# Hybrid decoder block, state-space stage: a second place for the input tile of the group products, and its load as a step of its own

## The chip, the cores and the metric

The kernel runs on one core of one Trainium2 chip. The metric is device time in microseconds (us) of one execution of the program; several executions are compared by their median.

## What is computed

One decoder block on x of shape 1 x 1024 x 1024 (float32) with a memory of 256 tokens. Two branches read one normalised input: a diagonal state-space recurrence in 32 groups of 16 channels, and an attention with forgetting. Sigmoid gates merge them. A projection, a cross-attention into the memory, a feed-forward layer and a last norm follow. Cut to what matters here:

```python
u = rms_norm(h, norm_mix[l])
proj = u @ w_in[l]
u_ssm, q, k, v, f_logit, gate_logits = jnp.split(proj, [...], axis=-1)
y_ssm = jax.nn.gelu(s5_ssm(u_ssm, lam_re[l], lam_im[l], log_dt[l], b_re[l], b_im[l],
                           c_re[l], c_im[l], d_skip[l]))
...
gate_a, gate_b = jnp.split(jax.nn.sigmoid(gate_logits), 2, axis=-1)
...
# s5_ssm: bu = b_bar * u per group, states by a linear recurrence over the sequence,
# y = Re(c * states) + d_skip * u
```

## The kernel before

Every large product is made of three TensorE products of a high and a low part of each factor (lines 168, 169 and 170), so that a product of two 1024-long factors for 128 output rows and 512 columns is 24 instructions. Weights come by a DMA from HBM into a tile `raw` and are split by ScalarE (`whi`, line 178) and VectorE or GpSimd (`wlo`, line 179).

The stage before this one (`stage_in`) makes the normalised input and the state-space input, and writes the latter to a DRAM tensor `u_d`, one piece for each quarter q of the 32 groups, out of SBUF tiles called `us` (line 435).

`stage_ssm` weaves two things. The main row is 32 gate products (`gate(j, h)`, 24 TensorE instructions each): their sums are passed through a sigmoid into one of two tiles `gs`, and stored to `gate_d` by a DMA that ScalarE issues (line 472). Their weights, a pair of `raw` tiles for every four gate products, are loaded by SP's DMA queue (line 153). Into this row the table `todo` puts the steps of the state-space part, four quarters q = 0 to 3, seven gate products apart:

- ahead of gate product 4 + 7q, `turn_weights(q)`: transposes of the weights `fre` and `fim` (line 1330) which ScalarE copies into `F` (line 1331), 8 small products (line 1336), and a tile `Ts` that is filled by three DMAs in a chain (line 1343).
- ahead of 5 + 7q, `states(q, u_d)`: it takes the one place of the tile `xg` (128 x 1024 float32, 512 KB), loads it from `u_d[q]` on SP's queue (line 1354) and multiplies it at once with `F` in 16 TensorE instructions (line 1361, two for each of eight groups). VectorE and GpSimd turn the result through a rotation, a scan and a rotation back into the states `St` (lines 1369 to 1390). GpSimd clears `St`'s first column (line 1384).
- in the same place `weights(q + 1)` prepares the next quarter's tables, most of it on GpSimd, the last doublings of `EC` and `ES` on VectorE (lines 1279 to 1320).
- ahead of 9 + 7q, `out(q)`: 32 instructions of `xg` with `Tt` (line 1404) and `St` with `Gm` (line 1405), GELU and a split, and `store(q)`: two DMAs to `y_d` (line 1413).

The tile `xg` is read twice, by `states(q)` and by `out(q)`; with one place, the next quarter's load can't start before `out(q)` has read it. The order in which each engine takes its instructions is fixed when the program is built. DMAs of one queue are issued by SP one after the other: an issue that waits for a semaphore holds up those behind it. The tiles of this stage lie in a pool `qp`, in memory that the tiles of `stage_in` (`xt`, `us` and others) held before: the first use of a tile waits for the last reader of what lay there.

Of the kernel before, what the change touches and what calls it, by code (L numbers as in the profile page):

```python
# [451 lines left out]
def stage_ssm(B, s5, qp, uT, w_in, gate_d, u_d, y_d):  # L452

    A, S = B.A, B.S
    s5.qp = qp
    w = {}

    def gate_weights(p):

        w[p] = [B.wblock(w_in, 4 * n, 4, C_G + 256 * p, 256) for n in range(2)]  # L460

    def gate(j, h):
        if h == 0 and j % 2 == 0 and j < 14:
            gate_weights(j // 2 + 1)
        ps = B.bank()
        o = j % 2 * P
        for k in range(8):
            wh, wl = [t_[:, k % 4, o:o + P] for t_ in w[j // 2][k // 4]]
            B.mm3(ps, wh, wl, *uT.rhs(k, h), k == 0, k == 7)
        gs = qp.tile([P, 512], F32, tag="gs", bufs=2, name="gs")  # L470
        mark.append(A.activation(gs, ps, AF.Sigmoid))
        A.dma_start(gate_d[j * P:(j + 1) * P, 512 * h:512 * h + 512], gs)

    def toeplitz():
        with B.tc.issue_after(mark[-1].ins):
            s5.toeplitz()

    def weights(q):
        with B.tc.issue_after(s5.doubled.ins):
            s5.weights(q)  # L480

    mark = []
    gates = [lambda j=j, h=h: gate(j, h) for j in range(16) for h in range(2)]
    gate_weights(0)
    s5.weights(0)
    todo = {}
    for q in range(4):
        todo[4 + 7 * q] = [lambda q=q: s5.turn_weights(q)]
        todo[5 + 7 * q] = [lambda q=q: s5.states(q, u_d)] + ([lambda q=q: weights(q + 1)] if q < 3 else [])
        todo[8 + 7 * q] = [toeplitz]  # L490
        todo[9 + 7 * q] = [lambda q=q: s5.out(q), lambda q=q: s5.store(q, y_d)]
    for i, f in enumerate(gates):
        for g in todo.get(i, []):
            g()
        f()
# [615 lines left out]
class S5:  # L1111
# [5 lines left out]
    def __init__(self, B, sp, lam_re, lam_im, log_dt, b_re, b_im, c_re, c_im, d_skip):  # L1117
        self.B, self.sp = B, sp
        self.raw = (lam_re, lam_im, log_dt, b_re, b_im, c_re, c_im, d_skip)

    def load(self, part):

# [132 lines left out]
    def t2(self, name, bufs=1):  # L1255
        return self.qp.tile([P, 512], F32, tag=f"q_{name}", bufs=bufs, name=name)
# [4 lines left out]
    def weights(self, q):  # L1261

        B, t2 = self.B, self.t2
        V, A, G = B.V, B.A, B.G
        j4 = slice(4 * q, 4 * q + 4)

        def bpow(tab, n):
            return tab[:, :n, j4].rearrange("p k j -> p j k").unsqueeze(3).to_broadcast([P, 4, n, 16])

        def bvec(v, n):  # L1270
            return v[:, j4, :].unsqueeze(2).to_broadcast([P, 4, n, 16])


        self.fb = [t2("fre"), t2("fim")]
        fv = [t_.rearrange("p (j t n) -> p j t n", j=4, t=8) for t_ in self.fb]
        w1, w2 = t2("w1"), t2("w2")
        w1v, w2v = [w[:, :448].rearrange("p (j t n) -> p j t n", j=4, t=7) for w in (w1, w2)]
        for o, (bx, by), op in ((0, (0, 1), ALU.subtract), (1, (1, 0), ALU.add)):
            G.tensor_tensor(out=w1v, in0=bpow(self.ld[0], 7), in1=bvec(self.bb[bx], 7), op=ALU.mult)
            G.tensor_tensor(out=w2v, in0=bpow(self.ld[1], 7), in1=bvec(self.bb[by], 7), op=ALU.mult)  # L1280
            G.tensor_tensor(out=fv[o][:, :, 0:7, :], in0=w1v, in1=w2v, op=op)
            G.tensor_copy(fv[o][:, :, 7, :], self.bb[o][:, j4, :])


        Gm = self.slot("Gm", 2)
        self.Gm = Gm.rearrange("p (g t m) -> p g t m", g=8, t=8)
        Gp = Gm.rearrange("p (j two t m) -> p j two t m", two=2, t=8, m=16)
        gv = [w.rearrange("p (j t m) -> p j t m", j=4, t=8) for w in (w1, w2)]
        for o in range(2):
            G.tensor_tensor(out=gv[0], in0=bpow(self.la[0], 8), in1=bvec(self.cT[o], 8), op=ALU.mult)  # L1290
            G.tensor_tensor(out=gv[1], in0=bpow(self.la[1], 8), in1=bvec(self.cT[1 - o], 8), op=ALU.mult)
            for two in range(2):
                h = slice(64 * two, 64 * two + 64)
                dst = Gp[64 * o:64 * o + 64, :, two]
                if o == 0:
                    V.tensor_sub(dst, gv[0][h], gv[1][h])
                else:
                    V.scalar_tensor_tensor(out=dst, in0=gv[0][h], scalar=-1.0, in1=gv[1][h],
                                           op0=ALU.mult, op1=ALU.subtract)


        EC, ES = [t2(n).rearrange("p (j c) -> p j c", j=4) for n in ("EC", "ES")]
        G.memset(EC[:, :, 0:1], 1.0)
        G.memset(ES[:, :, 0:1], 0.0)
        for k in range(7):
            n = 1 << k
            E = V if k > 4 else G
            bc = lambda tab: tab[:, 7 + k, j4].unsqueeze(2).to_broadcast([P, 4, n])
            for dst, (x1, x2), op in ((EC, (EC, ES), ALU.subtract), (ES, (ES, EC), ALU.add)):
                a1, a2 = [t2(s).rearrange("p (j c) -> p j c", j=4)[:, :, :n] for s in ("d1", "d2")]  # L1310
                E.tensor_tensor(out=a1, in0=x1[:, :, :n], in1=bc(self.cs), op=ALU.mult)
                E.tensor_tensor(out=a2, in0=x2[:, :, :n], in1=bc(self.sn), op=ALU.mult)
                done = E.tensor_tensor(out=dst[:, :, n:2 * n], in0=a1, in1=a2, op=op)
                if E is G:
                    self.doubled = done
        self.EC, self.ES = [e.rearrange("p j c -> p (j c)") for e in (EC, ES)]
        r8 = t2("r8")
        r8v = r8.rearrange("p (j c) -> p j c", j=4)
        A.copy(r8v, self.r8[:, j4].unsqueeze(2).to_broadcast([P, 4, P]))
        G.memset(r8v[:, :, 0:1], 0.0)  # L1320
        self.r8t = r8
# [25 lines left out]
        self.Tt = self.slot("Tt").rearrange("p (g t m) -> p g t m", g=8, t=8)  # L1347
        self.B.ordered = self.B.A.copy(self.Tt.rearrange("p g t m -> p t g m"), self.Ts)

    def states(self, q, u_d):  # L1350
        B, t2 = self.B, self.t2
        V, A, G, T, S = B.V, B.A, B.G, B.T, B.S
        self.xg = self.slot("xg").rearrange("p (g c) -> p g c", g=8)
        S.dma_start(self.xg, u_d[q].rearrange("t (n g) c -> (t n) g c", g=8))

        z = [t2("zre"), t2("zim")]
        zv = [t_.rearrange("p (j c) -> p j c", j=4) for t_ in z]
        for b in range(2):
            ps = B.bank("pv")
            for g in range(4):  # L1360
                T.matmul(ps[:, g * P:(g + 1) * P], self.F[:, 4 * b + g].rearrange("p r s -> p (r s)"),
                         self.xg[:, 4 * b + g, :], start=True, stop=True)
            pr = ps.rearrange("p (j two c) -> p j two c", j=2, two=2)
            for r in range(2):
                for two in range(2):
                    A.copy(zv[r][64 * two:64 * two + 64, 2 * b:2 * b + 2, :], pr[64 * r:64 * r + 64, :, two, :])

        a1, a2, a3, a4 = t2("m1"), t2("m2"), t2("m3"), t2("m4")
        V.tensor_mul(a1, z[0], self.EC)
        G.tensor_mul(a2, z[1], self.ES)  # L1370
        V.tensor_mul(a3, z[1], self.EC)
        V.tensor_mul(a4, z[0], self.ES)
        V.tensor_add(a1, a1, a2)
        V.tensor_sub(a3, a3, a4)
        sr, si = t2("zre"), t2("zim")
        V.tensor_tensor_scan(out=sr, data0=self.r8t, data1=a1, initial=0.0, op0=ALU.mult, op1=ALU.add)
        V.tensor_tensor_scan(out=si, data0=self.r8t, data1=a3, initial=0.0, op0=ALU.mult, op1=ALU.add)
        a1, a2, a3, a4 = t2("m1"), t2("m2"), t2("m3"), t2("m4")
        V.tensor_mul(a1, sr, self.EC)
        G.tensor_mul(a2, si, self.ES)  # L1380
        V.tensor_mul(a3, si, self.EC)
        V.tensor_mul(a4, sr, self.ES)
        self.St = self.slot("St").rearrange("p (g c) -> p g c", g=8)
        G.memset(self.St[:, :, 0:1], 0.0)
        Sv = self.St.rearrange("p (j two) c -> p j two c", two=2)
        for two in range(2):
            h = slice(64 * two, 64 * two + 64)
            v3 = lambda t_: t_[h].rearrange("p (j c) -> p j c", j=4)[:, :, 0:P - 1]
            V.tensor_sub(Sv[0:64, :, two, 1:P], v3(a1), v3(a2))
            V.tensor_add(Sv[64:128, :, two, 1:P], v3(a3), v3(a4))  # L1390
        self.use = (self.xg, self.Gm, self.St)
# [419 lines left out]
```

## Time and profile before

| | |
|---|---|
| three executions | 1586.69, 1590.88, 1595.57 us; median 1590.88 |
| profiled execution | span 1592.0 us from the first to the last instruction; no time of its own beside the span is given |
| TensorE busy | 1538.3 us, 97% of the span |
| VectorE, ScalarE, GpSimd busy | 1023.0, 655.8, 257.4 us |
| granted TensorE clock, mean | 0.984 |
| DMA | 240.86 MB, 151 GB/s over the span |
| state-space stage with the gate products | from about 108 to 328 us |

The profile is one execution, recorded by the hardware. A row of the timeline gives the start, the duration, the engine (PE is TensorE, DVE is VectorE, ACT ScalarE, POOL GpSimd; SPq and ACTq are DMA issues), the line of the kernel and the tiles, written first, then read; in brackets stands the idle time of the engine just before it and what ended it. Where an instruction waits for several semaphores, the one that came last by the profile is named. In rows of stretches, PEclk is the share of full clock that TensorE was granted.

### The profile page before, as it was taken

The numbers are of one execution on the slowest core, as the hardware profiler recorded it, in microseconds if no ns is written. First come the engines' busy times: TensorE is split into PE (matmuls) and PEld (weight loads), VectorE is DVE, ScalarE is ACT, GpSimd is POOL, SyncE is SP. The second block draws the span as 40 slices with busy tenths as digits, with TensorE's granted clock in tenths as the row PEclk, the third lists the DMA queues.
The fourth block names the chain that finished last, engine by engine and source line by source line (L and its number), as shares of the span: only waits on it lengthen the run. The fifth ranks groups of instructions, "written<-read, shape, count | busy, mean of one in ns | idle before, by whom it ended". The sixth has DMA issues, their size and how long they took to land.

```text
span 1592.0 us, 20434 instructions
## 1 busy us (share of the span) xinstructions
PE 1538.3 (97%) x7313; PEld 1265.5 (79%) x7313; DVE 1023.0 (64%) x1822; ACT 655.8 (41%) x1173; POOL 257.4 (16%) x339
## 2 busy tenths in 40 slices
PE   7799989999999899999999989999999999999997
PEld 6688878898777578878888778888888888788885
DVE  6756535444688777776455687777777775565555
ACT  6423334322566553232335564333333333354342
POOL 3037453200121114210001200010000000000001
PEclk8999999999999999999999999999999999999999
DMA  8763556332022746457403176555544443896542
GB/s 293 150 110 96 134 107 125 84 144 29 13 57 46 198 110 200 132 178 257 154 22 98 53 272 237 160 166 167 164 159 158 159 149 129 277 392 223 191 153 106
DMA packets 197941, 240.86 MB, mean 151 GB/s; under 512 B 35448, under 2 KB 126488, under 8 KB 197328
## 3 DMA queue, kind: packets, MB, share of 16 engines
q1 hardware_dynamic: 191216, 223.84, 47.7%
q10 hardware_dynamic: 6624, 15.73, 2.6%
q8 instruction: 57, 0.93, 0.2%
q14 instruction: 44, 0.36, 0.1%
HBM read 165.60 MB, written 75.86 MB: 152 GB/s over the span
## 4 chain that ended last, share of the span: by engine, by line
PE 79%; DVE 7%; DMA 6%; ACT 3%; POOL 2%; issue 2%; SPq 1%; DVEq 0%; POOLq 0%; ACTq 0%
PE mm L868 15%; PE mm L168 8%; PE mm L169 8%; PE mm L170 8%; PE pv L868 7%; PE mm L1005 4%; PE sc L868 4%; PE sc L168 3%; PE sc L170 3%; PE sc L169 3%; PE sc L1005 3%; PE pv L1005 3%; PE misc L1005 1%; DMA raw<-in_w_in_dram 1%; DMA raw<-in_w_mem_kv_dram 1%
## 5 line engine op out<-in xcount | busy, mean ns | idle before, releaser
L178 ACT CAST whi<-raw 128x1024 fp32r<-128x1024 f32 (+2 forms) x124 | 116.0, 941 | 178.0 <-PE mm L868 48.6
L179 DVE TENSOR_TENSOR wlo<-raw,whi 128x1024 fp32r<-128x1024 f32 (+2 forms) x121 | 130.9, 1086 | 75.2 <-ACT whi L178 73.1
L168 PE MATMUL mm<-uh,whi 128*128 128x512 f32 x344 | 138.5, 403 | 2.2 <-ACT whi L178 2.2
L170 PE MATMUL mm<-uh,wlo 128*128 128x512 f32 x344 | 135.9, 396 | 0.5 <-DVE wlo L179 0.5
L169 PE MATMUL mm<-ul,whi 128*128 128x512 f32 x344 | 136.4, 397 | 0.0
L179 DVE TENSOR_TENSOR ol<-or,oh 128x1024 fp32r<-128x1024 f32 x73 | 89.3, 1224 | 70.8 <-ACT oh L178 69.6
L178 ACT CAST oh<-or 128x1024 fp32r<-128x1024 f32 x73 | 76.8, 1053 | 103.3 <-PE mm L1005 35.2
L900 POOL TENSOR_TENSOR g<-a,c 128x512 f32<-128x512 f32 x22 | 35.3, 1603 | 392.8 <-ACT a L899 392.8
L197 POOL TENSOR_TENSOR r<-ms,mhalf 128x1 f32<-128x1 f32 (+1 forms) x30 | 17.9, 597 | 373.0 <-DVE ms L193 345.6
L168 PEld LDWEIGHTS mm<-uh,whi 128*128 128x128 f32 x344 | 66.0, 192 | 14.9 <-ACT whi L178 2.7
L170 PEld LDWEIGHTS mm<-uh,wlo 128*128 128x128 f32 x344 | 65.5, 190 | 14.9 <-DVE wlo L179 1.5
L1630 POOL TENSOR_TENSOR pl<-pf,ph 128x512 fp32r<-128x512 f32 (+1 forms) x32 | 37.8, 1181 | 244.5 <-DVE ph L1629 174.6
L169 PEld LDWEIGHTS mm<-ul,whi 128*128 128x128 f32 x344 | 65.8, 191 | 11.1
L1627 ACT ACTIVATE pf<-sc 128x512 f32<-128x512 f32 (+1 forms) x96 | 46.3, 489 | 44.9 <-DVE sc L1623 29.2
L868 PE MATMUL pv<-S3h,we 128*128 128x512 f32 x176 | 58.1, 389 | 0.0
L1633 DVE TENSOR_TENSOR pl<-pf,ph 128x512 fp32r<-128x512 f32 (+2 forms) x64 | 36.2, 567 | 10.1 <-ACT ph L1632 9.3
L1100 POOL TENSOR_TENSOR sg<-sg,ga 128x512 f32<-128x512 f32 x16 | 29.9, 1890 | 73.3 <-DVE sg L1093 73.0
L1005 PE MATMUL mm<-oh 128*128 128x512 f32 x106 | 41.2, 389 | 0.0
L1005 PE MATMUL mm<-ol,oh 128*128 128x512 f32 x106 | 41.2, 389 | 0.0
L1005 PE MATMUL mm<-oh,ol 128*128 128x512 f32 x106 | 41.2, 389 | 0.0
L168 PE MATMUL sc<-uh,whi 128*128 128x512 f32 x104 | 40.9, 393 | 0.0
L168 PE MATMUL mm<-yh,whi 128*128 128x512 f32 x104 | 40.7, 392 | 0.0
(579 smaller groups left out, 4558.3 us busy)
## 6 DMA issues: line engine op xcount, KB each, us to landing
or<-c_d SPq DMA_DIRECT2D x77, 256.0 KB
raw<-in_w_in_dram SPq DMA_DIRECT2D x22, 512.0 KB
wo<-in_w_ffn_out_dram SPq DMA_DIRECT2D x22, 512.0 KB
c_d<-g SPq DMA_DIRECT2D x44, 256.0 KB
t_d<-wo SPq DMA_DIRECT2D x44, 256.0 KB
or<-t_d SPq DMA_DIRECT2D x44, 256.0 KB
raw<-in_w_ffn_in_dram SPq DMA_DIRECT2D x20, 512.0 KB
rawb<-in_w_ffn_in_dram SPq DMA_DIRECT2D x20, 512.0 KB
```

Of the source, the lines that this page charges most:

```text
L168: T.matmul(ps, lh, rh, start=first, stop=False)
L169: T.matmul(ps, lh, rl, start=False, stop=False)
L170: T.matmul(ps, ll, rh, start=False, stop=last)
L178: self.A.copy(hi, src)
L179: (self.G if pool_lo else self.V).tensor_sub(lo, src, f32(hi))
L868: T.matmul(ps, l_[:, k, :], r_, start=first and k == 0 and i == 0, stop=k == 3 and i == 2, skip_group_check=True)
L900: G.tensor_mul(g[:, 512:], a1, c1)
L1005: T.matmul(ps, l_[:, gi], r_[:, 512:], start=n < 3 and p == 0 and k == 0 or n == 7 and p == 0 and k == 0, stop=p == NP - 1 and k == 2, ski ...
L1100: self.B.G.tensor_mul(self.out[j][:, cs], self.out[j][:, cs], ga)
L1627: self.exp = A.activation(pf[:, off:], ps[:, off:], AF.Exp)
L1630: G.tensor_sub(pl[:, off:], pf[:, off:], f32(ph[:, off:]))
L1633: V.tensor_sub(pl[:, off:], pf[:, off:], f32(ph[:, off:]))
```

## The change

The tile `xg` gets two places. Its load becomes a step `fetch(q)` of its own, which `todo` puts ahead of gate product 1 for q = 0 and ahead of gate product 6 + 7q for quarter q + 1, six gate products before `states(q + 1)`. `states` takes the tile that `fetch` left. No instruction of TensorE, VectorE, ScalarE or GpSimd is added or removed, and as many DMAs are issued as before.

```diff
     gate_weights(0)
     s5.weights(0)
-    todo = {}
+    todo = {1: [lambda: s5.fetch(0, u_d)]}
     for q in range(4):
         todo[4 + 7 * q] = [lambda q=q: s5.turn_weights(q)]
-        todo[5 + 7 * q] = [lambda q=q: s5.states(q, u_d)] + ([lambda q=q: weights(q + 1)] if q < 3 else [])
+        todo[5 + 7 * q] = [lambda q=q: s5.states(q)] + ([lambda q=q: weights(q + 1)] if q < 3 else [])
+        if q < 3:
+            todo[6 + 7 * q] = [lambda q=q: s5.fetch(q + 1, u_d)]
         todo[8 + 7 * q] = [toeplitz]
...
         self.raw = (lam_re, lam_im, log_dt, b_re, b_im, c_re, c_im, d_skip)
+        self.xgs = {}
...
-    def states(self, q, u_d):
+    def fetch(self, q, u_d):
+
+        self.xgs[q] = self.slot("xg", 2).rearrange("p (g c) -> p g c", g=8)
+        self.B.S.dma_start(self.xgs[q], u_d[q].rearrange("t (n g) c -> (t n) g c", g=8))
+
+    def states(self, q):
         B, t2 = self.B, self.t2
         V, A, G, T, S = B.V, B.A, B.G, B.T, B.S
-        self.xg = self.slot("xg").rearrange("p (g c) -> p g c", g=8)
-        S.dma_start(self.xg, u_d[q].rearrange("t (n g) c -> (t n) g c", g=8))
-
+        self.xg = self.xgs.pop(q)
```

Line numbers of the changed kernel are 3 higher from line 1120 on, and 6 higher behind `fetch`.

On SP, at quarters 0 and 1 (`xg_1376` and `xg_1792` are the tiles of q = 0 and q = 1, `raw` are gate weights, `us_648` is the last of the four `us` tiles), the queue stood so before:

```order
L435 DMA u_d_77<-us_648 128x8x128
L153 DMA raw_1616<-in_w_in_dram 128x4x256
L1354 DMA xg_1376<-u_d_77 128x1024
L153 DMA raw_1940<-in_w_in_dram 128x4x256
L153 DMA raw_1946<-in_w_in_dram 128x4x256
L1343 DMA Ts_1330<-Ts_1330 112x128
L1343 DMA Ts_1330<-Ts_1330 96x256
L1343 DMA Ts_1330<-Ts_1330 64x512
L153 DMA raw_2096<-in_w_in_dram 128x4x256
L153 DMA raw_2102<-in_w_in_dram 128x4x256
L1354 DMA xg_1792<-u_d_77 128x1024
L1413 DMA y_d_78<-yh_1650 128x1024
```

and in the changed kernel, where `xg_1224`, `xg_1552` and `xg_1980` are the tiles of q = 0, 1 and 2:

```order
L1356 DMA xg_1224<-u_d_77 128x1024
L1356 DMA xg_1552<-u_d_77 128x1024
L153 DMA raw_1940<-in_w_in_dram 128x4x256
L153 DMA raw_1946<-in_w_in_dram 128x4x256
L1346 DMA Ts_1332<-Ts_1332 112x128
L1346 DMA Ts_1332<-Ts_1332 96x256
L1346 DMA Ts_1332<-Ts_1332 64x512
L153 DMA raw_2098<-in_w_in_dram 128x4x256
L153 DMA raw_2104<-in_w_in_dram 128x4x256
L1356 DMA xg_1980<-u_d_77 128x1024
L1419 DMA y_d_78<-yh_1652 128x1024
```

The load of q = 0 has kept its place. That of q = 1 follows it directly, and where it stood before, behind two pairs of weight loads, that of q = 2 stands now.

On SP one quarter later, before, with `xg_2220` the tile of q = 2:

```order
L153 DMA raw_2396<-in_w_in_dram 128x4x256
L153 DMA raw_2402<-in_w_in_dram 128x4x256
L153 DMA raw_2552<-in_w_in_dram 128x4x256
L153 DMA raw_2558<-in_w_in_dram 128x4x256
L1354 DMA xg_2220<-u_d_77 128x1024
L1413 DMA y_d_78<-yh_2066 128x1024
```

and in the changed kernel, with `xg_2396` the tile of q = 3:

```order
L153 DMA raw_2398<-in_w_in_dram 128x4x256
L153 DMA raw_2404<-in_w_in_dram 128x4x256
L153 DMA raw_2554<-in_w_in_dram 128x4x256
L153 DMA raw_2560<-in_w_in_dram 128x4x256
L1356 DMA xg_2396<-u_d_77 128x1024
L1419 DMA y_d_78<-yh_2068 128x1024
```

The load in this place is now that of the last quarter, and the place where `xg_2648` (q = 3) stood before, a quarter later, is empty.

On GpSimd, in the preparation of quarter 0 (`weights(0)`; what an instruction waits for stands in brackets, Pool_49 is GpSimd's own work), before:

```order
L1311 TENSOR_TENSOR d1_1111<-EC_1107,trg_cs_867 128x4 [waits Pool_49]
L1312 TENSOR_TENSOR d2_1112<-ES_1108,trg_sn_866 128x4 [waits Pool_49]
L1384 MEMSET St_1420 128x8
L1339 MEMSET Ts_1758 128x896
L1281 TENSOR_TENSOR fim_1087<-w1_1088,w2_1089 128x4x112 [waits Pool_49]
L1313 TENSOR_TENSOR EC_1107<-d1_1111,d2_1112 128x4 [waits Pool_49]
```

and in the changed kernel:

```order
L1314 TENSOR_TENSOR d1_1111<-EC_1107,trg_cs_867 128x4 [waits Pool_49]
L1315 TENSOR_TENSOR d2_1112<-ES_1108,trg_sn_866 128x4 [waits Pool_49]
L1390 MEMSET St_1420 128x8 [waits DMAHW4_49]
L1342 MEMSET Ts_1760 128x896
L1284 TENSOR_TENSOR fim_1087<-w1_1088,w2_1089 128x4x112 [waits Pool_49]
L1316 TENSOR_TENSOR EC_1107<-d1_1111,d2_1112 128x4 [waits Pool_49]
```

The order is the same, but the first clearing of `St` has a wait that it had not: the second place of `xg` has moved the tiles behind it in the pool, `St` lies now where `us_648` lay, and DMAHW4_49 tells of the landing of the store of that tile to `u_d`. No other engine's order differs between the two kernels.

## The prediction

> **What bounds the kernel now.** First the page: how busy each engine is, and the chain of waits.
>
> ```profile
> span 1592.0 us, 20434 instructions
> ...
> PE 1538.3 (97%) x7313; PEld 1265.5 (79%) x7313; DVE 1023.0 (64%) x1822; ACT 655.8 (41%) x1173; POOL 257.4 (16%) x339
> ...
> PE 79%; DVE 7%; DMA 6%; ACT 3%; POOL 2%; issue 2%; SPq 1%; DVEq 0%; POOLq 0%; ACTq 0%
> ```
>
> TensorE is the bound, and time is to be had only where it stands still or runs at a reduced clock. So next its waits in the stretch from 100 to 330 us, the stage that the change touches (engine and line, whom it waited for, us in total, times, longest):
>
> ```profile
> PE pv L1361 <- DMA xg<-u_d: 4.9, 1, 4.9
> PE pv L1361 <- ACT whi L178: 0.9, 1, 0.9
> ```
>
> These are all its waits there, and both stand ahead of line 1361, the first products of `xg`. TensorE's timeline around the four quarters' products:
>
> ```profile
> 136.81 1.95 PE L1361 MATMUL pv<-xg,F 128*128 128x128 f32 x16
> ...
> 184.11 2.02 PE L1361 MATMUL pv<-xg,F 128*128 128x128 f32 x16 [0.95 <-ACT whi L178]
> ...
> 191.46 0.39 PE L168 MATMUL mm<-uh,whi 128*128 128x512 f32 x1
> ...
> 230.16 0.39 PE L170 MATMUL mm<-uh,wlo 128*128 128x512 f32 x1
> 235.43 3.75 PE L1361 MATMUL pv<-xg,F 128*128 128x128 f32 x16 [4.89 <-DMA xg<-u_d]
> ...
> 245.61 0.39 PE L168 MATMUL sc<-uh,whi 128*128 128x512 f32 x1
> ...
> 284.56 1.95 PE L1361 MATMUL pv<-xg,F 128*128 128x128 f32 x16
> ```
>
> Quarters 0 and 3 start with no gap, quarter 1 after 0.95 us, quarter 2 after 4.89. When were the loads issued?
>
> ```profile
> 108.45 0.37 SPq L435 DMA_DIRECT2D u_d<-us  x1
> ...
> 116.01 0.34 SPq L1354 DMA_DIRECT2D xg<-u_d  x1
> ...
> 172.38 1.51 SPq L153 DMA_DIRECT2D raw<-in_w_in_dram  x2
> 173.98 0.46 SPq L1354 DMA_DIRECT2D xg<-u_d  x1
> ...
> 218.07 1.50 SPq L153 DMA_DIRECT2D raw<-in_w_in_dram  x2
> 219.66 1.21 SPq L1354 DMA_DIRECT2D xg<-u_d  x1
> ...
> 265.48 0.34 SPq L1354 DMA_DIRECT2D xg<-u_d  x1
> ```
>
> From issue of `xg` to first product: 20.8, 10.1, 15.8 and 19.1 us. In quarters 1 and 2 the load is issued right behind two weight loads of 512 KB each, and the product starts as it lands; the chain of waits says so for quarter 2:
>
> ```profile
> 219.66 15.63 DMA xg<-u_d
> ```
>
> For quarter 1 the page names a ScalarE cast `whi`. The product doesn't read that tile. What it needs of ScalarE is `F`, done at 178.41 + 0.59 = 179.00, 4 us before the gap:
>
> ```profile
> 178.41 0.59 ACT L1331 COPY F<-pv 128x512 f32<-128x512 f32 x1 [2.29 <-DMA raw<-in_w_in_dram]
> ```
>
> So I take the 0.95 us as the load too. Last, the clock behind the long gap (stretch, its length, busy time of PE, PEld, DVE, ACT, POOL; then granted clock, DMA share, GB/s):
>
> ```profile
> 230.00:234.00 4.00, 0.54 (x3) 0.12 (x1) 1.37 (x2) 0.60 (x1) 2.44 (x3) 1.00 0.96 193
> ...
> 236.00:240.00 4.00, 4.00 (x18) 3.81 (x18) 0.92 (x3) 2.20 (x7) 0.00 (x0) 0.50 0.58 213
> ```
>
> After the gap TensorE runs at half speed.
>
> **The change part by part.** *The loads move ahead.* The load of q = 1 goes out behind that of q = 0, at about 116.4 us, and is used at 183: some 67 us, against 15.8 for the slowest seen. That of q = 2 takes the place at 173.98 and is used at 230.5 (56 us), that of q = 3 the place at 219.66, used near 276 (56 us). Each place waits, as before, for the `out` that reads its predecessor. Both gaps go: 4.89 + 0.95 = 5.84 us.
>
> *The clock.* From the first product of a quarter to the start of the second gate product behind it, TensorE took 245.61 - 235.43 = 10.18 us in quarter 2 and 191.46 - 184.11 = 7.35 in quarter 1, for the same 16 + 24 instructions. Without the gap there is nothing to lower the clock: 2.83 us.
>
> *The added load at 116 us.* What lies behind it on SP is a pair of weight loads and then `Ts`; that pair is held by weight splits on VectorE until 134.67, so SP has 18 us to spare. On the DMA engines:
>
> ```profile
> 109.00:136.00 27.00, 27.00 (x133) 22.75 (x132) 11.35 (x18) 6.61 (x9) 23.63 (x49) 1.00 0.54 108
> ```
>
> ```profile
> 134.67 4.09 DVE L179 TENSOR_TENSOR wlo<-raw,whi 128x1024 fp32r<-128x1024 f32 x2
> ```
>
> 46% of 27 us are free, 12 us of all engines, and 512 KB at the 108 GB/s of that row is 4.9 us, at the 213 of the row above 2.5. The stores of the gates share the engines; each has two gate products (2 x 5.4 us) until its `gs` is written again. I take 0; with no cover it would be 2.5 to 4.9.
>
> *The new wait on GpSimd.* The clearing of `St` now waits for the store of the last `us` tile. In this trace the load of q = 0 was released by that store (first row, of SP's waits), and issued at 116.01; the other rows are of GpSimd and VectorE:
>
> ```profile
> SPq L1354 <- DMA u_d<-us: 6.4, 1, 6.4
> ```
>
> ```profile
> 112.02 0.11 POOL L1384 MEMSET St<- 128x8 f32 x1
> ...
> 131.34 1.16 POOL L1281 TENSOR_TENSOR fre<-w,w 128x448 f32<-128x448 f32 x1 [2.04 <-PE misc L1336]
> ```
>
> ```profile
> 140.83 1.38 DVE L1296 TENSOR_TENSOR Gm<-w,w 64x512 f32<-64x512 f32 x2 [1.87 <-POOL w L1291]
> ```
>
> The store, issued at 108.45, landed at about 115.9, so GpSimd stops at 112.0 for 3.9 us, and all that is queued behind is late by as much: `fim`, which is needed only at 129, the doublings of `EC` and `ES`, and the next quarter's `fre`. There GpSimd has a pause of 2.04 us; 1.9 remain. VectorE, which takes the last doublings from GpSimd, has one of 1.87 ahead of `Gm`; 2.0 remain. Both then run into the states of q = 0:
>
> ```profile
> 157.53 0.69 DVE L1390 TENSOR_TENSOR St<-m,m 64x508 f32<-64x508 f32 x1
> ```
>
> ```profile
> 161.05 0.39 PE L1405 MATMUL pv<-St,Gm 128*128 128x128 f32 x2
> ```
>
> The last part of `St` is done at 158.22 and needed at 161.05, the second product of `St`; 2.8 us to spare (the first product needs only half of `St`, which is ready earlier). A delay of 2.0 fits under 2.8: cost 0. If the pauses absorbed nothing, 3.9 - 2.8 = 1.1. The next pause, ahead of the transposes of q = 1, takes up the rest.
>
> *What is late next.* At quarter 0, with no gap, `St` is ready 158.22 - 136.81 = 21.4 us after the states' first product, and needed after 24.2. Quarter 2 without its gap has that margin, 2.8 us. Gate weights next, a split on VectorE and the product that uses it:
>
> ```profile
> 260.46 1.22 DVE L179 TENSOR_TENSOR wlo<-raw,whi 128x1024 fp32r<-128x1024 f32 x1
> ```
>
> ```profile
> 270.96 0.39 PE L168 MATMUL mm<-uh,whi 128*128 128x512 f32 x1
> ```
>
> This split is done at 261.68; its gate product started at 270.96 and moves to 262.3 if TensorE comes 8.7 us earlier. It would just be in time even if VectorE came no earlier at all. Later stages follow TensorE's pace, and their loads move with it.
>
> *Sum:* 4.89 + 0.95 + 2.83 + 0 + 0 = 8.67 us. The span goes from 1592.0 to 1583.3. The span is 1.1 us above the median of the runs shown (no time of that execution is given beside its span); applied to the median, 1590.88 - 8.67 = **1582.2 us**, 0.54% less. About 0.5% (7.95 us, at 1582.9) is what a measurement of this kernel can tell from no change.
>
> **The rivals.** *No clock term.* The fall to 0.50 may not follow the gap in every run. In this trace much shorter gaps, 0.81 and 0.62 us, were followed by a slow stretch, which speaks for keeping the term:
>
> ```profile
> 380.15 0.44 PE L1593 MATMUL mm<-hb 68*128 68x384 f32 x1 [0.81 <-ACT hb L1568]
> ...
> 381.21 0.65 PE L1593 MATMUL mm<-hb 68*128 68x512 f32 x1 [0.62 <-DVE mc L1595]
> ```
>
> ```profile
> 381.40:384.80 3.40, 3.40 (x8) 2.43 (x8) 2.29 (x7) 0.00 (x0) 0.00 (x0) 0.50 0.02 5
> ```
>
> Without it 5.84 are left: 1585.0. Behind this stands a rule: the Trainium skill (TensorE: Matmul & The Clock Gate, Part 1: The HAM clock gate) has the clock halved after at least one idle window of about 3.4 us, and the window runs free, so that one kernel is slowed differently from run to run; by it 4.89 us hold a whole window in fewer than half of the runs. The rows above disagree, since neither gap is that long.
>
> *The gap is that of this one execution.* How late the tile of q = 2 comes hangs on two weight loads. Had it taken the 10.1 us of quarter 1, it would have landed at 229.8, before 230.5: no gap, no lowered clock. The runs shown spread over 8.9 us, about the size of my sum, which speaks for it; that the profiled one lies near the median speaks against. Gains between 0.95 (if other runs have only quarter 1's gap) and 5.84: 1585 to 1590, middle 1587.5.
>
> *More than the sum.* Other slow stretches depend on where short gaps fall. TensorE 8.7 us earlier shifts them all. The one at 381 costs 3.40 / 2 = 1.7; that one and another like it gone too would make 3.4: 1578.8. As many may be added, which leads to the case before.
>
> *Slower.* GpSimd's new wait ends with a store to DRAM. If that lands later than here, the delay L passes the pauses: from L = 2.04 + 2.83 = 4.9 us on TensorE waits at 161 for `St`, one for one, and behind a gap like that of quarter 2 the clock drops, another 2.83. To eat up 8.67, L must be over 4.9 + 5.8 = 10.7, with the store landing at 123. Issued at 108.45, it would have to take as long as the slowest load here (15.8 us gives 124.3, L = 12.3): 1590.88 - 8.67 + 7.4 + 2.8 = 1592.4. Against it: the trace has L = 3.9, and a single weight load just ahead of that store, not two.
>
> A second rule only makes this case dearer: the Trainium skill (SBUF — State Buffer, "SBUF: two separate sides") has VectorE and GpSimd take one port pair in turns, each blocked for the other's whole instruction. The pushed instructions meet others than before, at most a us or two each way; it changes no term while the 2.8 us hold.
>
> *The change doesn't do what it says:* a load of q = 1 that is itself held on SP. Its one new wait is for TensorE work of the stage before, and TensorE, which works in order, was in the gate products by 110; so it isn't. I give it no chance of its own.
>
> **How the numbers follow.** Forecast as summed, 1579.5 to 1584.5: 0.56. No clock term, 1585.0: 0.08. A smaller gap in other runs, 1585 to 1590: 0.16. More, around 1578.8: 0.12. Slower than before: 0.08. The likeliest time is 1582.2. The range reaches from the "more" case, with 2 us for the scatter of a median, to the far end of the smaller gap: 1576.5 to 1590. Faster by over 0.5% means below 1582.9, which cuts through the forecast's own range 0.7 us above its middle; I give 0.42 of its 0.56 to that side, because the terms that I left at 0 are small and the scatter above is partly in the other cases. With the 0.12: 0.54. Within 0.5%: 0.14 + 0.08 + 0.16 + 0.02 = 0.40. Slower by over 0.5%: 0.06.
>
> **What would show it.** In the new profile: the four groups of line 1367 (the moved 1361) with no idle time ahead; clock 1.00 from 225 to 250; `xg` issued at about 116.0, 116.4, 174 and 220; GpSimd's clearing of `St` at 116 instead of 112; the first `St` products at 160.6 with no gap; `out(2)` some 8.7 us earlier. Wrong if TensorE waits for `St` or a weight split in a place where it didn't, or if the gap at quarter 2 proves to be absent from most executions before.

## The result, and the profile after

The changed kernel takes **1584.91 us** (median of 21 runs, 1581.64 to 1589.25), the kernel before beside it 1590.98 (21 runs, 1586.69 to 1595.57). The ratio is 0.9966, 95% interval 0.9957 to 0.9975: 6.07 us faster, 4.0 to 6.8 by the interval. The forecast was 1582.2 with a range of 1576.5 to 1590.0, and 8.67 us of gain. The direction held and the time lies in the range; but 0.34% is on the "within 0.5%" side, to which 0.40 was given, and the size was overestimated by 2.6 us. The profiled execution took 1585.95 us. From its page (span, busy time, the chain of waits):

```profile
span 1584.2 us, 20431 instructions
...
PE 1533.6 (97%) x7313; PEld 1261.6 (80%) x7313; DVE 1022.7 (65%) x1822; ACT 655.2 (41%) x1173; POOL 254.1 (16%) x339
...
PE 80%; DVE 7%; DMA 6%; ACT 3%; POOL 2%; issue 1%; SPq 1%; DVEq 0%; POOLq 0%; ACTq 0%
```

All waits of TensorE from 100 to 330 us in the changed kernel:

```profile
PE pv L1410 <- ACT Tt L1351: 0.2, 1, 0.2
```

Both waits for `xg` are gone, and a new one is there, for another tile: `Tt`, ahead of line 1410 (the moved 1404), the first products of `out(0)`. TensorE's first products of `F` in the four quarters, and SP's issues of the loads:

```profile
138.46 1.95 PE L1367 MATMUL pv<-xg,F 128*128 128x128 f32 x16
...
185.22 1.95 PE L1367 MATMUL pv<-xg,F 128*128 128x128 f32 x16
...
231.42 1.95 PE L1367 MATMUL pv<-xg,F 128*128 128x128 f32 x16
...
277.59 1.95 PE L1367 MATMUL pv<-xg,F 128*128 128x128 f32 x16
```

```profile
117.18 0.81 SPq L1356 DMA_DIRECT2D xg<-u_d  x2
...
178.86 0.46 SPq L1356 DMA_DIRECT2D xg<-u_d  x1
...
221.96 0.46 SPq L1356 DMA_DIRECT2D xg<-u_d  x1
```

No row of the first fence has an idle time in brackets; the loads of quarters 1 to 3 go out 53 to 68 us ahead of their use (that of quarter 2 about 3 us later than forecast, behind weight loads that wait for VectorE). TensorE's clock in the place where it had fallen to 0.50 (the columns are those of the stretches in the prediction; the share of the clock is the third number from the end):

```profile
231.00:235.00 4.00, 4.00 (x27) 3.63 (x26) 1.37 (x2) 0.60 (x1) 2.44 (x3) 1.00 0.88 210
```

From the first product of quarter 0 to that of quarter 3 is 284.56 - 136.81 = 147.75 us before and 277.59 - 138.46 = 139.13 now: 8.62 us, almost exactly the 8.67 of the sum. So the question is not where the gain went within these two traces, but why the medians are only 6.07 apart.

### The profile page after: what moved, and what is told of

Read it like the earlier page. It is cut to its first block, busy times and chain, and to the rows that moved or that the text cites. A ratio compares the mean times of both kernels' runs of the same rounds, so it can differ in the third digit from the quotient of the medians.

```text
span 1584.2 us, 20431 instructions
## 1 busy us (share of the span) xinstructions
PE 1533.6 (97%) x7313; PEld 1261.6 (80%) x7313; DVE 1022.7 (65%) x1822; ACT 655.2 (41%) x1173; POOL 254.1 (16%) x339
## 4 chain that ended last, share of the span: by engine, by line
PE 80%; DVE 7%; DMA 6%; ACT 3%; POOL 2%; issue 1%; SPq 1%; DVEq 0%; POOLq 0%; ACTq 0%
PE mm L870 15%; PE mm L168 8%; PE mm L169 8%; PE mm L170 8%; PE pv L870 7%; PE mm L1007 4%; PE sc L870 4%; PE sc L1007 3%; PE sc L168 3%; PE sc L170 3%; PE sc L169 3%; PE pv L1007 3%; PE misc L1007 1%; DMA raw<-in_w_in_dram 1%; DMA raw<-in_w_mem_kv_dram 1%
```

## The experiments

One measure runs through all of them: the distance between the first `F` products of neighbouring quarters, read from rows like the four above. A quarter without any wait takes 46.2 us. The stretch behind quarter 3, up to the next stage's first product, took 73.2 us in every trace, so these three distances are the whole difference in the stage from quarter 0's first product on (which itself came at 136.1 to 139.3 us). Gains are medians against the kernel before on the same chip.

| kernel | q0 to q1 | q1 to q2 | q2 to q3 | sum | median us | gain us | ratio (95%) |
|---|---|---|---|---|---|---|---|
| before, profile of the prediction | 47.30 | 51.32 | 49.13 | 147.75 | | | |
| before, second profile | 47.14 | 50.31 | 47.93 | 145.38 | | | |
| before, third | 47.15 | 50.37 | 47.93 | 145.45 | | | |
| before, fourth | 47.10 | 50.33 | 47.90 | 145.33 | | | |
| the change | 46.76 | 46.20 | 46.17 | 139.13 | 1584.91 | 6.07 | 0.9966 (0.9957-0.9975) |
| the change, again | 47.46 | 46.17 | 46.20 | 139.83 | 1586.15 | 5.23 | 0.9967 (0.9955-0.9979) |
| two places alone | 47.48 | 46.19 | 46.18 | 139.85 | 1585.74 | 5.41 | 0.9959 (0.9945-0.9973) |
| change without GpSimd's wait | 46.20 | 46.17 | 46.19 | 138.56 | 1583.53 | 7.62 | 0.9948 (0.9932-0.9964) |
| the same, again | 46.18 | 46.19 | 46.18 | 138.55 | 1583.15 | 8.23 | 0.9948 (0.9935-0.9962) |
| only quarter 2 early | 47.30 | 46.27 | 46.20 | 139.77 | 1584.72 | 6.43 | 0.9956 (0.9941-0.9970) |
| only quarter 1 early | 46.19 | 51.24 | 48.37 | 145.80 | 1589.95 | 1.15 | 0.9988 (0.9977-1.0000) |
| GpSimd's wait alone | 50.04 | 47.87 | 46.19 | 144.10 | 1591.08 | 0.30 | 0.9994 (0.9983-1.0005) |
| gap filled | 46.25 | 51.11 | 46.18 | 143.54 | 1589.87 | 1.51 | 0.9988 (0.9977-1.0000) |
| load on ScalarE's queue | 46.19 | 46.18 | 46.19 | 138.56 | 1585.04 | 6.06 | 0.9956 (0.9940-0.9973) |

**Is the gap that of one execution?** The kernel before, unchanged, was profiled three more times.

> The kernel before, unchanged, profiled once more, to see whether the gaps are those of one execution. Theory A (the gaps are there every time): TensorE waits for the input tile ahead of the products of F in quarters 1 and 2, about 1 and 4.9 us, and runs at 0.50 for some microseconds behind the second. Theory B (the median gain of 6.1 us is smaller than the stage's 8.6 in the profile because the gap of quarter 2 is smaller in most executions): the gap of quarter 2 is under 3 us or gone.

> The kernel before, unchanged, profiled a third time. Theory A (the gaps and the clock behind them are worth 8.7 us every time): gaps of 5.8 us in all, low clock of 5 to 6 us behind them. Theory B (the profile on which the prediction rests was one of the worse executions): gaps of 3 to 5 us in all, and one low stretch of 3.4 us.

> The kernel before, unchanged, profiled a fourth time, with the same two expectations as the third: gaps of 5.8 us and low clock of 5 to 6 us (Theory A), or gaps of 3 to 5 us in all and one low stretch of 3.4 us (Theory B).

All three read alike; the gap of quarter 2 lies between the two expectations of the second profile, and the third and fourth, whose expectations were written after it, came out as theory B says. The waits of the second profile, its first product of quarter 2, and the clock behind it:

```profile
PE pv L1361 <- DMA xg<-u_d: 4.7, 2, 3.9
```

```profile
185.92 2.02 PE L1361 MATMUL pv<-xg,F 128*128 128x128 f32 x16 [0.80 <-DMA xg<-u_d]
...
236.23 3.63 PE L1361 MATMUL pv<-xg,F 128*128 128x128 f32 x16 [3.90 <-DMA xg<-u_d]
```

```profile
236.40:239.80 3.40, 3.40 (x17) 3.40 (x17) 1.37 (x2) 1.47 (x4) 0.92 (x1) 0.50 0.79 310
```

The gap of quarter 2 is 3.9 us, not 4.89, and the low clock lasts 3.4 us. Its cost, by the distance from quarter 2 to 3, is 47.93 - 46.18 = 1.75 us, not 2.83. Of four traces of the kernel before, the one on which the prediction was built is the worst in this stage, by 2.3 us, and the other three agree within 0.12. Both waits are put down to the load of `xg` here, quarter 1's too: the ScalarE cast that the first profile named was indeed not it, and with only that load early (below) the gap is gone.

**Does the separate step matter, or the place alone?**

```diff
-        self.xg = self.slot("xg").rearrange("p (g c) -> p g c", g=8)
+        self.xg = self.slot("xg", 2).rearrange("p (g c) -> p g c", g=8)
```

> The kernel before with two places for the input tile and nothing else: the load stays in the code of the states, no step of its own. Its instructions come out in the same order as in the changed kernel. Theory A (the place alone does it): no wait for the input tile from 100 to 330 us, and 5 to 7 us faster than before, as the changed kernel. Theory B (the separate step does part of it): at least 2 us less gain than the changed kernel's 6.1.

It gains 5.41 us, as the change does. The scheduler, which takes a load as early as its place allows, issues all loads where the change has them (67.5, 52.5 and 56.2 us ahead of their use). The step of its own and its six gate products of lead add nothing.

**What does GpSimd's new wait cost?** The change once more, and the change with the second place under another name, so that it lies behind `St` in the pool and the clearing of `St` no longer waits for the last store of `us`:

```diff
-        self.xgs[q] = self.slot("xg", 2).rearrange("p (g c) -> p g c", g=8)
+        self.xgs[q] = self.slot(("xg", "xh")[q % 2]).rearrange("p (g c) -> p g c", g=8)
```

> The changed kernel with the second place under a name of its own, so that it is laid out behind St and the clearing of St on GpSimd does not wait for the store of the last us tile; the order of the loads is that of the changed kernel. Theory A (the pauses of GpSimd and VectorE take up that wait, cost 0): the gap of 3.4 us ahead of the clearing is gone from GpSimd, and the time is within 0.5 us of the changed kernel's, 6 us faster than before. Theory B (the new wait costs the difference between the stage's gain and the median's): 1 to 2.5 us faster than the changed kernel.

> The changed kernel once more, beside the three others. Expected 5 to 7 us faster than before. Theory A (the wait on GpSimd makes VectorE late, and TensorE then waits for Tt in quarter 0): a wait for Tt of 0.2 to 1 us at about 162 in its trace, as in the first profile of the change (0.2) and in the kernel with two places alone (0.9). Theory B (that wait costs nothing): no wait of TensorE at all from 100 to 330 us.

> The changed kernel without the wait on GpSimd, once more, side by side with the changed kernel. Theory A (the wait for Tt costs TensorE 0.2 to 1 us, and a lowered clock behind it where there is one): 0.5 to 2.5 us faster than the changed kernel. Theory B (the 2.2 us between this kernel and the one with two places alone were spread of the runs): within 0.4 us of it.

The second profile of the change has the wait for `Tt` again, longer:

```profile
PE pv L1410 <- ACT Tt L1351: 0.9, 1, 0.9
```

The two kernels with both places side by side show it in three of three traces (0.2, 0.9 and 0.9 us), the one without GpSimd's wait in none of two. In the column q0 to q1 it is 46.76, 47.46 and 47.48 against 46.20 and 46.18: the wait costs 0.6 to 1.3 us. In all four traces with GpSimd's wait (these three and the one of the next experiment) the copy of `Tt` is done 23.6 to 24.6 us behind quarter 0's first product, in the ten without it after 20.6, and TensorE can use it after 23.57. How it comes about is seen on three engines of the changed kernel's first trace, of which quarter 0 begins 138.46 - 136.81 = 1.65 us later than before. GpSimd:

```profile
117.16 0.11 POOL L1390 MEMSET St<- 128x8 f32 x1 [3.44 <-DMA u_d<-us]
```

VectorE, which takes the last doublings of `EC` and `ES` from GpSimd; its twelve instructions in a stretch before, and the same twelve after (third busy time: VectorE, fifth: GpSimd):

```profile
127.40:134.60 7.20, 7.20 (x46) 6.34 (x45) 6.96 (x12) 2.53 (x4) 5.16 (x7) 1.00 0.11 39
```

```profile
132.60:143.20 10.60, 10.60 (x58) 9.11 (x58) 10.36 (x12) 3.73 (x10) 8.96 (x10) 1.00 0.14 51
```

They begin 3.5 us late (132.54 against 127.38, less 1.65) and take 3.4 us longer. The sizes are the same; what differs is who works beside them. The first of these rows and two more before, the same three after, and GpSimd's rows beside the last two:

```profile
127.38 1.07 DVE L1311 TENSOR_TENSOR d<-EC,trg_cs 128x128 f32<-128x128 f32 x1 [2.19 <-POOL ES L1313]
...
129.49 0.29 DVE L1313 TENSOR_TENSOR EC<-d,d 128x128 f32<-128x128 f32 x1
...
130.67 0.42 DVE L1311 TENSOR_TENSOR d<-EC,trg_cs 128x256 f32<-128x256 f32 x1
```

```profile
132.54 1.06 DVE L1314 TENSOR_TENSOR d<-EC,trg_cs 128x128 f32<-128x128 f32 x1 [2.18 <-POOL ES L1316]
...
134.64 1.20 DVE L1316 TENSOR_TENSOR EC<-d,d 128x128 f32<-128x128 f32 x1
...
138.27 1.31 DVE L1314 TENSOR_TENSOR d<-EC,trg_cs 128x256 f32<-128x256 f32 x1
```

```profile
134.53 1.15 POOL L1284 TENSOR_TENSOR fre<-w,w 128x448 f32<-128x448 f32 x1
...
138.16 1.14 POOL L1284 TENSOR_TENSOR fim<-w,w 128x448 f32<-128x448 f32 x1
```

Before, GpSimd stood still from 129.3 to 131.3, in the pause of 2.04 us of the prediction; now it works through, and each of VectorE's instructions that begins beside one of its products ends about where that ends. So the pause that took up GpSimd's delay had been the time in which VectorE ran unhindered. From ScalarE, before and after:

```profile
152.50 0.62 ACT L1319 COPY r<-R 128x512 f32<-128x512 f32 x1 [7.65 <-DVE zim L1377]
...
156.41 1.04 ACT L1348 COPY Tt<-Ts 128x1024 f32<-128x1024 f32 x1
```

```profile
157.38 0.62 ACT L1322 COPY r<-R 128x512 f32<-128x512 f32 x1 [10.88 <-DVE zim L1383]
...
161.29 1.03 ACT L1351 COPY Tt<-Ts 128x1024 f32<-128x1024 f32 x1
```

ScalarE's copy of `r` waits for VectorE, 4.88 - 1.65 = 3.23 us later than before, and behind it in ScalarE's queue stands, with no idle time between, the copy of `Tt`. Before, `Tt` was ready at 157.45 and needed at 160.38: 2.93 us to spare. 3.23 - 2.93 = 0.3 us is TensorE's delay (from the first `F` product to the first `Tt` product it is 23.91 us, 0.34 more than before).

The kernel without that wait has the lowest medians: 3.0 us under the change beside it, more than the 0.5 to 2.5 expected. But the intervals of the two ratios overlap, and the kernel with the load on ScalarE's queue (below), whose stage is as short, gains no more than the change. Only 0.6 to 1.3 us of the 3.0 lie in the stage's distances. The remainder is spent outside of them, where the order of TensorE's instructions is the same, and it isn't shown that the wait causes it: from quarter 3's first product to the end, the four traces of the kernel before took 1303.4 to 1308.4 us, the two of the change 1306.7 and 1306.4, these two 1303.9 and 1304.0, and these two are each the fastest of their kernel's six executions.

**The same wait put into the kernel before**, by an empty place behind `xg`; no load moves:

```diff
-        self.xg = self.slot("xg").rearrange("p (g c) -> p g c", g=8)
+        self.xg = self.slot("xg").rearrange("p (g c) -> p g c", g=8); q == 0 and self.slot("pad")
```

> The kernel before, with an empty place of the tile's size laid out behind the input tile: St lies where the last us tile lay, as in the change, and the clearing of St waits for that tile's store; no load moves. Theory A (the wait is not free): TensorE waits for Tt in quarter 0, and the kernel is 0.5 to 2.5 us slower than before. Theory B (the pauses take it up, cost 0): within 0.4 us of before. In both the waits for the input tile in quarters 1 and 2 stay.

No cost can be measured here: 0.30 us less by the medians, ratio 0.9994 with an interval of 0.9983 to 1.0005. Theory A missed, and so did the sentence that both gaps would stay:

```profile
187.93 2.47 PE L1361 MATMUL pv<-xg,F 128*128 128x128 f32 x10 [3.35 <-DMA xg<-u_d]
```

The gap of quarter 1 is 3.35 us in that trace, and quarter 2 has none. VectorE's delay is there as well, but it reached TensorE by another way: the weight loads ahead of `xg` on SP wait for splits on VectorE, so the load of quarter 1 went out 178.05 - 137.89 = 40.2 us behind quarter 0's first product, against 173.98 - 136.81 = 37.2 before.

```profile
178.05 0.46 SPq L1354 DMA_DIRECT2D xg<-u_d  x1
```

TensorE, later by that gap, then found the load of quarter 2 landed. So in this trace the delay moved a wait from one place to another, while with early loads it is added to a stage that has no other wait.

**Which of the two loads carries the gain?** Two places by name, so that only one load is freed:

```diff
-        self.xg = self.slot("xg").rearrange("p (g c) -> p g c", g=8)
+        self.xg = self.slot("xg" if q < 2 else "xh").rearrange("p (g c) -> p g c", g=8)
```

and, for the other kernel, `q < 1`.

> Two places by name, the first for quarters 0 and 1, the second for 2 and 3: only the load of quarter 2 goes early (at 116 us), those of 1 and 3 are issued where they were before. Theory A (the terms of the prediction): the gap of quarter 1 stays, about 1 us, the gap of quarter 2 and the low clock behind it are gone, 4.89 + 2.83 = 7.7 us in the profile. Theory B (the gap of quarter 2 is only part of it in most executions): 3 to 5 us faster in the median. Rival C (the early load of quarter 1, with the second load at 116 us, carries the gain): no faster than 1 us.

> Two places by name, the first for quarter 0, the second for 1, 2 and 3: only the load of quarter 1 goes early (at 116 us), those of 2 and 3 are issued where they were before. Theory A (the terms add up): the gap of quarter 1 is gone, that of quarter 2 and the low clock behind it stay; 0 to 2 us faster than before. Theory B (the gaps stand in for each other: TensorE that is not held up in quarter 1 reaches quarter 2 earlier, while the load there is no earlier): the gap of quarter 2 is longer than 4.9 us, and the time is within 1 us of before. Rival C (quarter 1 carries the gain): 3 us faster or more.

Quarter 2's load alone brings 6.43 us, between the 7.7 of its theory A and the 3 to 5 of theory B, and its trace keeps the gap of 0.95 us at quarter 1. Quarter 1's load alone brings 1.15, with an interval that reaches to none. In the trace of the latter, the stretch that holds the gap of 4.9 us and what followed:

```profile
PE pv L1361 <- DMA xh<-u_d: 4.9, 1, 4.9
```

```profile
231.60:238.40 6.80, 4.29 (x18) 4.23 (x19) 1.66 (x3) 1.96 (x6) 2.16 (x2) 0.50 0.78 301
```

TensorE comes 0.95 us earlier to quarter 2 (46.19 against 47.14), the load does not, and the gap there is 4.9 us, against 3.9 in three of the four traces before: what is saved at quarter 1 is waited for at quarter 2. The terms don't simply add.

**Is the low clock caused by the gap?** In the kernel before, TensorE was kept busy with products that nobody reads while it waits for the load of quarter 2 (`lastmm` is the last gate product ahead of it; the line that sets it is left out here):

```diff
+        if q == 2:
+            with B.tc.issue_after(B.lastmm.ins):
+                B.warm(44)
```

> The kernel before with 44 products of 128x256 that nobody reads, placed on TensorE ahead of the first products of the input tile in quarter 2, so that TensorE is busy while it waits for that load. The load is as late as before. Theory A (the lowered clock behind the gap is caused by the gap and is a term of its own): the wait of 4 to 5 us is replaced by the idle products, the clock behind them stays 1.00, and the kernel is 1.7 to 2.8 us faster than before. Theory B (the clock falls whatever stands there): the same time as before, or slower by what the products take beyond the gap.

```profile
229.04 4.98 PE L241 MATMUL misc<-ident 128*128 128x256 bf16 x44
...
233.85 1.95 PE L1364 MATMUL pv<-xg,F 128*128 128x128 f32 x16
```

```profile
229.00:234.00 5.00, 5.00 (x47) 4.49 (x47) 1.37 (x2) 0.60 (x1) 3.44 (x4) 1.00 0.99 350
234.00:238.00 4.00, 4.00 (x28) 3.60 (x27) 2.07 (x3) 2.93 (x8) 0.15 (x1) 1.00 0.36 135
```

The clock stays at 1.00. Against the trace with only quarter 1 early, whose stretch of 4.9 us is idle instead, quarter 2 to 3 takes 46.18 instead of 48.37 us: 2.2 us are the clock's, and they hang on the gap. The median gains 1.51 us, near 1.75; its interval of 0 to 3.7 excludes neither no gain nor the 2.83 of the sum, so it is the traces that show the term. (Three instructions of ScalarE and two of GpSimd also changed places in this kernel.)

**Place or queue?** The kernel before with its one place, and the load issued by ScalarE instead of SP:

```diff
-        S.dma_start(self.xg, u_d[q].rearrange("t (n g) c -> (t n) g c", g=8))
+        A.dma_start(self.xg, u_d[q].rearrange("t (n g) c -> (t n) g c", g=8))
```

> The kernel before with one place, the load issued on ScalarE's queue instead of SP's; there it stands right behind ScalarE's last work on the out of the quarter before, and no weight load is ahead of it in its queue. Theory A (what makes it late is its place behind two weight loads of SP's queue): both gaps are gone or under 1 us in all, 4 to 7 us faster. Theory B (what makes it late is the DMA engines, which the weight loads keep busy whatever the queue, or the one place, which comes free too late): a gap of 2 us or more stays in quarter 2, under 3 us faster.

ScalarE's issues:

```profile
164.12 0.33 ACTq L1354 DMA_DIRECT2D xg<-u_d  x1
...
210.31 0.33 ACTq L1354 DMA_DIRECT2D xg<-u_d  x1
...
256.48 0.33 ACTq L1354 DMA_DIRECT2D xg<-u_d  x1
```

With one place the load of quarter 2 goes out at 210.31, when `out(1)` is done with it, where SP issued it at 219.66. That is 18 us ahead of its use at 228.45, and no wait of TensorE is left. What held SP, from 185 to 236 us before:

```profile
SPq L153 <- DVE wlo L179: 27.7, 3, 24.7
```

A weight load ahead of `xg` in SP's queue waits 24.7 us for a split on VectorE. So it is the place in the queue that made the load late; the second place in memory is one way past it, and not the only one.

## Why the prediction was right in kind and too large in size

- *The gaps go, and the clock with them*: right. Both waits, and the low clock behind the long one, are gone in every trace with early loads, and filling the gap shows the clock's term by itself.
- *4.89 and 2.83 us*: the terms that were mis-sized. They measured 4.89 and 2.83 in one execution; in the three others the gap of quarter 2 is 3.9 us and the clock costs 1.75. The step that failed is "that the profiled one lies near the median speaks against" the rival of a gap of this one execution. A span near the median says nothing on one stage: the second profile has a span of 1590.9 us, and its stage is 2.4 us shorter. That rival, with a chance of 0.16 and 1585 to 1590, came nearest in its mechanism, though it assumed that with a smaller gap no low clock would be left. By the number, "no clock term" came nearest (1585.0 against 1584.91), which is luck, since the clock term is there.
- *0.95 us at quarter 1*: right cause, but not gained in the change. The wait for `Tt` takes its place: the change's q0 to q1 is 46.76 or 47.46 where it was 47.1 to 47.3, and the kernel in which only quarter 2 is early is as fast as the change.
- *GpSimd's new wait, 0*: it measured 0.6 to 1.3 us in the stage. The delay was well estimated (3.9 us; 3.44 and 4.25 in the two traces), and GpSimd's pause did take up its part. Two things failed: VectorE's own delay grew by 3.4 us, because GpSimd's pause had been its undisturbed time, and the tile that TensorE waited for was not `St` but `Tt`, whose copy waits in ScalarE's queue and had 2.93 us to spare. (`St` was as late: done 24.6 us behind quarter 0's first product instead of 21.4, just when it was needed.) The prediction's sign of being wrong, a wait for `St`, missed it. The sentence on VectorE and GpSimd, "at most a us or two each way; it changes no term while the 2.8 us hold", was too low: the delay was 3.4 us, and the 2.8 didn't hold. The Trainium skill (SBUF — State Buffer, "SBUF: two separate sides"), named there, says that of a GpSimd instruction and a VectorE one with two inputs in SBUF, whichever begins first blocks the other for its whole instruction; the rows agree (1.20 us beside a product of GpSimd that ends at 135.68, 0.29 without).
- *The added load at 116 us, 0*: right; without GpSimd's wait no wait of TensorE is left from 100 to 330 us, with that load in place.
- *No clock term, by a whole idle window of 3.4 us*: six gaps of 3.35 to 4.9 us were recorded (four traces of the kernel before, one with GpSimd's wait alone, one with only quarter 1 early), and each was followed by a low stretch, so this rival is out. Of the Trainium skill's rule (TensorE: Matmul & The Clock Gate, Part 1: The HAM clock gate) the free-running window agrees with the traces (last section), but not that a whole window must be idle: by it, as an estimate, a gap of 3.9 us would hold a window of 3.4 in one case of seven, and one of 3.35 in none. In these traces TensorE was still busy for 3 to 10% of the step that ended with the fall, behind the gaps of 3.35 and 3.9 us, and for 29% with only quarter 1 early.
- *Together*: a typical trace before has 145.4 us, the change 139.1 to 139.85: 5.6 to 6.3 us, which is near the 6.07 measured. Against the single trace of the prediction it would be 8.6. That it agrees to some tenths is partly luck: in other rows of the table the gain of the median and that of the distances are up to 1.5 us apart (8.23 against 6.9, 1.15 against -0.4).

## What to carry to other kernels

A stage's gap should be read from several profiles before it is priced: a span near the median doesn't make each stage of that execution a typical one. A load that comes late in an in-order queue is first moved past what it waits behind, here by another queue or by a place of its own; where a new place lands in memory decides what new waits come with it, and the version with the lowest medians here differs from the change only in that. And idle time of one engine is not a free cushion when another engine runs faster in it: the delay has to be followed through every queue that hangs on it.

## What the runs showed of the hardware

- The granted clock changes in steps of 3.41 us: every low stretch but the one that runs past the program's end lasts a multiple of that, and within one trace all of them begin whole steps apart (with two places alone at 373.39, 520.17 and 943.42 us, which is 43 and 124 steps). Gaps of 3.35 and 3.9 us were followed by 3.4 us at 0.50. Those of 4.9 were followed by 6.8, of which the first 0.8 and 2.5 us still lie in the gap. The two gaps of 0.81 and 0.62 us in a later stage were followed by a low stretch in 5 of 14 traces and by none in 9, at the same place of the program. In the kernel with two places alone, and in the second profile of before:

```profile
373.40:376.80 3.40, 3.40 (x8) 2.43 (x9) 2.33 (x7) 0.00 (x0) 0.00 (x0) 0.50 0.02 4
```

```profile
381.40:384.80 3.40, 3.40 (x15) 2.72 (x16) 2.50 (x8) 0.00 (x0) 0.00 (x0) 1.00 0.00 0
```

  What differs is where the steps fall. In the first of these traces both gaps lie in one step, in the second the end of a step parts them; the steps with the most idle time (first busy time: TensorE):

```profile
369.98:373.39 3.41, 1.97 (x14) 1.52 (x12) 1.60 (x6) 1.55 (x3) 0.00 (x0) 1.00 0.45 53
```

```profile
376.32:379.73 3.41, 2.60 (x22) 2.40 (x21) 1.38 (x2) 1.91 (x5) 0.00 (x0) 1.00 0.52 48
```

  In the five traces with a low stretch TensorE was busy for 56 to 58% of that step, in the nine without for 60 to 77%. That is no threshold for other places: elsewhere a few steps with 43 to 48% were followed by none. So a low stretch behind a short gap hangs on where the steps fall in that execution, is worth about 1.7 us, and adds to the spread of the runs (8.9 us in the first three).
- VectorE's instructions on 128x128 and 128x256 elements took 0.29 and 0.42 us with GpSimd idle, and 1.20 and 1.31 beside a GpSimd product.
